# A two-layer hybrid decoder trunk on one core: the SBUF pools laid out anew, so that weights, work slots and x tiles begin at multiples of 512 bytes

## Chip, cores and metric

One NeuronCore of a Trainium2 chip. The metric is the device time of one execution in microseconds (us), lower is better. The input is one sequence of 512 tokens with 1024 channels in float32, through two layers.

## What is computed

```python
c_act = jax.nn.silu(c)
for layer in range(DEPTH):                                   # 2
    mod = jnp.einsum('bd,de->be', c_act, w_mod[layer]) + b_mod[layer]
    shift1, scale1, gate1, shift2, scale2, gate2 = split(mod, 6)
    h = rms_norm(x, mix_norm_w[layer]) * (1.0 + scale1) + shift1
    proj = jnp.einsum('btd,de->bte', h, w_in[layer])
    y_a = deltanet_mixer(...); y_b = spatial_gating_mixer(...); y_c = dilated_attention_mixer(...)
    x = x + gate1 * jnp.einsum('bte,ed->btd', concat(y_a, y_b, y_c), w_out[layer])
    h = rms_norm(x, ffn_norm_w[layer]) * (1.0 + scale2) + shift2
    gate, up = split(jnp.einsum('btd,df->btf', h, w_ffn_in[layer]), 2)
    x = x + gate2 * jnp.einsum('btf,fd->btd', jax.nn.silu(gate) * up, w_ffn_out[layer])
```

## The kernel before

x lies transposed in SBUF: eight tiles `xs` of [128 channels, 512 tokens]. Every operand of a large matmul is kept as two float32r parts, high (rounded) and low (the rest), and one product takes three matmuls: high by high, high weights by low x, low weights by high x. `mm3` (lines 548 to 552) issues these three, always in this order, on one bank of PSUM. A weight block is 128x128 and is the stationary operand; it is loaded anew before each of the three matmuls. The moving operand is a [128, 512] part of x.

Weights come from HBM in pieces, nearly all of [128, 1024], that is eight blocks of 128 columns (512 bytes per partition each). `loader` (line 429) issues their DMAs on SyncE into a ring of four `raw` tiles. `splitter` (line 473) makes the parts: ScalarE copies a piece to a `hi` tile, VectorE writes the difference to a `lo` tile. `hi` and `lo` are rings of three buffers each, so piece after piece goes round the three. `wcols` (line 513) picks a block of a piece. A few pieces, those for which `piece` has a `loose` number, are split into work slots instead of the ring.

Work slots are 58 equal tiles of [128, 512] float32 (`Arena`, line 240). They hold the parts of x, the results on their way, and everything else of that size. In a projection (`group`, `channels`) the moving operand is a slot and the stationary one a block of a ring buffer. In `proj_n` (line 1401) it is the other way round: a token block of a slot is stationary and 512, 256 or 264 columns of a ring buffer are moving. In `last_tiles` (line 652) both are slots, and the moving operand is half a slot, 256 columns.

The order of the instructions is made by a planner: tasks run against a rough model of the engines' time, and each engine's instructions are noted in that order. All have the source line 233. Names of tiles: `w` is a slot, `hi`, `lo`, `raw` the rings, `cst` the constants, `b` a PSUM bank, `s` a small tile. The profile writes a matmul as `b<-moving,stationary`.

Where the tiles lie follows from the order of the pools and the sizes of their tiles. In the program before, the pool `keep` (x, constants) comes first, then `par` (small tiles), then the slots and the rings. The slots begin at byte 62,112 of a partition and are 2,048 bytes apart, so every slot begins 160 bytes beyond a multiple of 512. A buffer of a ring is as large as its largest piece (1,056 columns, 4,224 bytes, that is 128 bytes more than a multiple of 512), so the three buffers differ:

| buffer of the ring | `hi` begins at, mod 512 | `lo` begins at, mod 512 | a slot begins at, mod 512 |
|---|---|---|---|
| first | 160 | 32 | 160 |
| second | 288 | 160 | 160 |
| third | 416 | 288 | 160 |

Blocks inside a piece are 512 bytes apart, so all blocks of a buffer have its offset. The constants begin at 128 mod 512.

Of the kernel before, what the change touches and what calls it, by code (L numbers as in the profile page):

```python
# [9 lines left out]
F32 = mybir.dt.float32  # L10
# [7 lines left out]
P = 128  # L18
T = 512
D = 1024  # L20
# [8 lines left out]
# columns of the constants array  # L29
C_ID, C_ONES, C_TRIU, C_TRIL, C_SLOW, C_BD, C_M64, C_M128, C_MG0, C_MPI, C_COS, C_SIN, C_RM = (  # L30
    0, 128, 256, 384, 512, 640, 768, 896, 1024, 1280, 1536, 1600, 1664)
C_N = 1665

# columns of the per-layer parameters array
L_BMOD, L_NW, L_CONV, L_ALOG, L_DTB, L_ONW, L_WC, L_RW, L_RWS = 0, 48, 64, 112, 116, 120, 121, 123, 155
L_N = 187

N_SLOTS = 58
N_RAW, N_RING = 4, 3
# [6 lines left out]
# the ranks of the tasks in layer 0 and after (the lowest goes first), the slack of an engine's queue, the free slots that  # L46
# weights kept apart from the ring ask for, and the banks that a projection leaves free
# [16 lines left out]
# the projections in the order of the mixers' use (in layer 0, k and q come first), and their pieces of w_in  # L64
# [9 lines left out]
# The kernel is written as tasks (generators), which run against a rough model of the engines' time, so that each  # L74
# engine's instructions come in an order in which few have to wait. A task yields what its next step needs: an AP
# (its data written), a Flag or Task (done), a function (time, or None while unknown), a tuple of these, or None.
# [10 lines left out]
class Plan:  # L87
# [21 lines left out]
    @staticmethod  # L109
    def span(ap):  # L110
        """the name of an AP's tensor, and its first and last column"""
        (step, _), free = ap.ap[0], ap.ap[1:]
        lo = ap.offset % step if ap.space != bass.MemoryType.DRAM and step else 0
        return ap.tensor.name, lo, lo + sum((n - 1) * s for s, n in free)
# [108 lines left out]
class Engine:  # L223
    """an engine whose instructions are noted in the plan"""
# [15 lines left out]
class Arena:  # L240
    """Equal tiles, the one that has been free longest first."""
# [22 lines left out]
    def need(self, n):  # L264
        """what a task yields that needs n of them"""
        return lambda: self.free[n - 1][0] if len(self.free) >= n else None


class Pair:
    """the float32 parts (high, low) of a [128, 512] operand; ok: written, by halves of the tokens"""  # L270
# [11 lines left out]
def _trunk(ctx, tc, xT, cb, consts, prm, gmp, wmod, wt, wn, wab, wo, wo2, wf1, wf2, out):  # L282
# [5 lines left out]

    keep = ctx.enter_context(tc.tile_pool(name="keep", bufs=1))
    par = ctx.enter_context(tc.tile_pool(name="par", bufs=1))  # L290
    wk = ctx.enter_context(tc.tile_pool(name="wk", bufs=1))
    wp = ctx.enter_context(tc.tile_pool(name="wp", bufs=4))
# [11 lines left out]
    def slots(n, spare=0):  # L304
        """n slots, as soon as they and some more are free"""
        yield arena.need(n + spare)
        return [slot() for _ in range(n)]

    def bank(n=1, spare=0):
        """n banks of psum, as soon as they and some more are free"""  # L310
        yield banks.need(n + spare)
        got = [banks.get() for _ in range(n)]
        return got[0] if n == 1 else got
# [14 lines left out]
    def heads(ap, n, w):  # L328
        """[128, n] as [128, n, w], each value w times"""
        return ap.rearrange("p (h o) -> p h o", o=1).to_broadcast([P, n, w])  # L330

    def every(ap, n, w):
        """[128, w] as [128, n, w], n times"""
# [45 lines left out]
    # pieces in the order of their use: columns of w_mod, and weights, which are split into float32 parts  # L379
# [5 lines left out]
    for l in range(depth):  # L385
# [9 lines left out]
        for k, (w, i) in enumerate(p for name in ORDER[min(l, 1)] for p in PIECES[name]):  # L395
            piece(w, l, i, 4 * 264 if w == "ab" else 1024, LOOSE["t"] if w == "t" and i < 3 else 0)
# [24 lines left out]
    def ring(tag, n, dt, bufs):  # L421
        t = wp.tile([P, n], dt, tag=tag, name=nm(tag), bufs=bufs)
# [4 lines left out]
        return t  # L427
# [25 lines left out]
    def modulation():  # L453
        """the entries of the modulation, in the order of their weights"""
# [44 lines left out]
    def take(*key):  # L499
        """the parts of the next weights"""  # L500
# [12 lines left out]
    def wcols(w, j, n=128):  # L513
        if isinstance(w[0], list):
            return wcols((w[0][j * n // T], w[1][j * n // T]), j % (T // n), n)
        return w[0][:, j * n:(j + 1) * n], w[1][:, j * n:(j + 1) * n]
# [5 lines left out]
    def rsqrt(v, n):  # L522
        """v ** -0.5 on [128, n] (v > 0): an integer start, then a step of third and one of second order"""
# [12 lines left out]
    def split(src, pair):  # L536
        """the float32 parts of a slot, which is freed"""
# [10 lines left out]
    def mm3(ps, w, x, first, last):  # L548
        """ps += w.T @ x by the float32 parts; w, x: (high, low)"""
# [4 lines left out]
    def operand(x, cols):  # L554
        """waits for an operand's columns"""
# [5 lines left out]
    def group(ws, rhs, cols, pss, order=range(KC)):  # L561
        """pss[j] = j-th weights.T @ rhs, chunk by chunk"""
# [6 lines left out]
    def tile_t(key, rhs):  # L569
        """psum of one column tile"""  # L570
# [6 lines left out]
    def tiles_t(keys, rhs):  # L577
        """psums of some column tiles together, by halves of the tokens"""
# [10 lines left out]
    def inv_rms(a, b0, n, warm=None):  # L589
        """psum with the inverse rms of x in every row, for n blocks of tokens from b0"""  # L590
# [17 lines left out]
    def norm_half(a, h, gg, l, which, half):  # L608
        """h = (high, low) of rms_norm(x) * w * (1 + scale) + shift, for half of the tokens"""
# [25 lines left out]
    def residual(c, ps, gate, cols, a):  # L635
        """x += gate * ps, and its squares"""
# [12 lines left out]
    def last_tiles(cs, w, where, rhs, gates, before, a, l, which):  # L649
        """the last chunks of a projection to x, by halves of the tokens, each with the norm that follows;  # L650
        returns its parts. where(c, k): which of the weights w, and which of its columns"""
# [34 lines left out]
    def conv(ps, ti, cw, func):  # L686
        """silu of the causal convolution of a projection, from psum; func: Silu, or Tanh and halved taps in cw
        (which needs no other table than Exp)"""
# [17 lines left out]
    def sumsq_heads(tiles):  # L706
        """[128 tok, (blk, h)] of the sums of squares over the 128 channels of each head, plus EPS"""
# [23 lines left out]
    def gates(ab, pr):  # L731
        """ab: [128, blk, 8] with a (4), b (4); returns g and beta, [128, (blk h)]"""
# [15 lines left out]
    def decay(c, g):  # L748
        """exp of the sums of g between the tokens of chunk c, lower triangles, (h, 128)"""
# [13 lines left out]
    def triangle(c, kT, s1, E, bc4):  # L763
        """B, the strictly lower part of the chunk's system (its upper part isn't zero)"""
# [17 lines left out]
    def blocks(l, bc, Bs):  # L782
        """inverses of the 32 x 32 diagonal blocks of I + B, compact: [128, (chunk h), 32]"""
        yield tuple(Bs)
        yield bc
        # one diagonal block per partition, forward substitution on the identity
        Q.dma_start(out=bscr[l].rearrange("n b i j -> (b i) n j"), in_=bc.rearrange("p (n j) -> p n j", j=32))
        free(bc)
        # and one half of the columns of its inverse: the even ones, the odd ones
# [28 lines left out]
    def dn_attn(c, qT, kT, E, B):  # L818
        """transposes of the decayed products of queries and keys of chunk c"""
# [21 lines left out]
    def dn_values(vT, h, bv):  # L841
        """beta * |k|^-1 * v of one head, [128 tok, (chunk, 128)]"""
# [15 lines left out]
    def dn_inverse(c, B, xc):  # L858
        """transposes of (I + B)^-1 of chunk c"""
# [39 lines left out]
    def k_decayed(c, kT, eg):  # L899
        """keys of chunk c, [128 tok, (h, 128)], decayed to its end"""  # L900
# [9 lines left out]
    def dn_chunk_out(c, qT, vt, AT, St, eg, oss):  # L910
        """o of chunk c, [128 tok, (h, 128)], and the sums of its squares"""
# [28 lines left out]
    def dn_scan(qT, kT, vv, Rs, ATs, scales, oss):  # L940
        """returns the tasks of o per chunk"""
# [64 lines left out]
    def dn_norm(scan, oss, qss):  # L1006
        """o is q.(rest) without the query's norm: its scale, rsqrt(|q|^2 + EPS) / sqrt(128), goes into the EPS"""
# [33 lines left out]
    def gmlp(l, vg):  # L1041
        """vg: two slots of gelu(v), [128 tok, (2 blk, 256)]; returns what gelu(u) is multiplied by, transposed"""
# [44 lines left out]
    def gated(l, ub, ts, pair, h_done):  # L1087
        """pair = gelu(u) * what the other half gives for it"""
# [12 lines left out]
    def rope_tables(pr):  # L1101
        """cos * w and sin * w (halves exchanged, first negative) for q and k; columns for the other channels"""
# [12 lines left out]
    def sw_in(b, ps, ss):  # L1115
        """a block of q and k from psum, and the sums of squares of its heads"""
# [11 lines left out]
    def sw_qk(xin, ss, gi, tables):  # L1128
        """four blocks [128 tok, q 256 | k 256]; returns -q.T / 8 per head pair and k.T per head, zero padded;
        patterns 1, 2: tokens in the order of t % 4"""  # L1130
# [93 lines left out]
    def attention(part, qk, vals, ml):  # L1224
        """part 0: blocks of tokens in order, keys of the block before and its own, pattern 0;
        part 1: blocks of one residue of t % 4, keys of the block for pattern 1 and for pattern 2.
        Scores are negated. ml: (minimum, sum) [128, (b h 2)]; returns the unnormalised outputs, transposed,
        per head pair"""
# [26 lines left out]
    def merge(l, mls, atts, pairs, last):  # L1255
        """one softmax over the keys of all patterns. (minimum, sum) go to the other part's order of tokens:
        token = 128 b + p in part 0, 4 p + r in part 1"""
# [57 lines left out]
    def first():  # L1315
        """layer 0: h chunk by chunk as the modulation comes, and with it the projections of k and q"""
# [4 lines left out]
        def warm(t, n=1):  # L1321
            """the tensor engine's clock rises with its load"""
# [62 lines left out]
    def layer(l, h, kq):  # L1385
        """the mixers; returns what goes into the channel mixer"""
# [14 lines left out]
        def proj_n(keys, width, tok):  # L1401
            """psum per block of tokens, [128 tok, width]; keys: (key, chunks of d in it)"""
            pss = None
            k = 0
            for key, n in keys:
# [3 lines left out]
                for j in range(n):  # L1409
                    wj = wcols(w, j, width)  # L1410
# [70 lines left out]
        def scales_of(gt, kss):  # L1481
            """decays to and from each token and over each chunk; beta / |k|, beta / |k|^2, and its product"""
# [106 lines left out]
        # output projection  # L1589
# [142 lines left out]
def _pack(inp):  # L1732
# [18 lines left out]
        rep(qw[:, :16]), rep(kw[:, :16]), rep(qw[:, swap]), rep(kw[:, swap]),  # L1751
    ], axis=2)
# [13 lines left out]
    # in layer 0, k and q run together: a piece per chunk of d  # L1766
# [32 lines left out]
```

## Time and profile before

| | |
|---|---|
| time, median of 3 runs | 1504.33 us (1503.94 to 1507.3) |
| span of the profiled execution | 1501.6 us |
| TensorE (PE) busy | 1478.1 us, 98% of the span, 7810 matmul records |
| weight loads (PEld) busy | 1235.6 us, 82% |
| VectorE (DVE) busy | 886.5 us, 59% |
| ScalarE (ACT) busy | 593.2 us, 40% |
| mean granted TensorE clock | 0.998 |
| DMA | 178.96 MB, queue busy 36.6% of 16 engines |

The profiled execution is known by its span alone, from its first to its last instruction; it lies 2.7 us below the median of the times. A matmul's duration in the profile is from its start to its modelled end, and one begins before the other has ended, so the pace of TensorE is read from starts, not from durations. An fp32 matmul has two records, an fp32r one has one; a row that says "f32" gives the type as the record has it, for both.

### The profile page before, as it was taken

The numbers are of one execution on the slowest core, as the hardware profiler recorded it, in microseconds if no ns is written. First come the engines' busy times: TensorE is split into PE (matmuls) and PEld (weight loads), VectorE is DVE, ScalarE is ACT, GpSimd is POOL, SyncE is SP. The second block draws the span as 40 slices with busy tenths as digits, with TensorE's granted clock in tenths as the row PEclk, the third lists the DMA queues.
The fourth block names the chain that finished last, engine by engine and source line by source line (L and its number), as shares of the span: only waits on it lengthen the run. The fifth ranks groups of instructions, "written<-read, shape, count | busy, mean of one in ns | idle before, by whom it ended". The sixth has DMA issues, their size and how long they took to land.

```text
span 1501.6 us, 19988 instructions
## 1 busy us (share of the span) xinstructions
PE 1478.1 (98%) x7810; PEld 1235.6 (82%) x7810; DVE 886.5 (59%) x1836; ACT 593.2 (40%) x1047; POOL 41.6 (3%) x60
## 2 busy tenths in 40 slices
PE   7999999999999999999999999999999999999998
PEld 5777998888988888888897889978788888888887
DVE  7787887946855555555476787656476333333332
ACT  4484326574432212222345623546544222122221
POOL 0001000000000000000000300100000000000000
PEclk9999999999999999999999999999999999999999
DMA  8723443404166555555322232121141223222231
GB/s 292 258 78 112 128 152 120 142 19 150 61 216 186 186 189 195 185 187 175 110 92 75 67 108 55 43 85 36 52 141 57 92 90 98 98 89 94 98 106 49
DMA packets 70638, 178.96 MB, mean 119 GB/s; under 512 B 25104, under 2 KB 25744, under 8 KB 70544
## 3 DMA queue, kind: packets, MB, share of 16 engines
q1 hardware_dynamic: 70544, 177.69, 36.6%
q8 instruction: 61, 1.00, 0.3%
q14 instruction: 33, 0.27, 0.1%
HBM read 174.45 MB, written 3.21 MB: 118 GB/s over the span
## 4 chain that ended last, share of the span: by engine, by line
PE 97%; DVE 1%; DMA 1%; ACT 1%; issue 0%; SPq 0%; ACTq 0%; DVEq 0%
PE b L233 97%; DMA raw<-in_wt_dram 0%; ACT w L233 0%; DVE w L233 0%; DMA xs<-in_xT_dram 0%; DVE raw L233 0%; SPq L233 0%; DVE s L233 0%; DVE xs L233 0%; ACT hi L233 0%; DVE lo L233 0%; DVE mod L233 0%; ACTq L233 0%; DVEq L233 0%
## 5 line engine op out<-in xcount | busy, mean ns | idle before, releaser
L233 PE MATMUL b<-w,hi 128*128 128x512 f32 (+1 forms) x2748 | 854.1, 392 | 2.5 <-ACT w L233 1.6
L233 PEld LDWEIGHTS b<-w,hi 128*128 128x128 f32 x2748 | 512.0, 189 | 123.8 <-issue 6.7
L233 PE MATMUL b<-w,lo 128*128 128x512 f32 (+1 forms) x1374 | 540.4, 393 | 0.0
L233 ACT ACTIVATE hi<-raw 128x1024 fp32r<-128x1024 f32 (+2 forms) x215 | 222.3, 1036 | 617.8 <-PE b L233 420.5
L233 DVE TENSOR_TENSOR lo<-raw,hi 128x1024 fp32r<-128x1024 f32 (+2 forms) x215 | 257.7, 1200 | 268.0 <-ACT hi L233 264.9
L233 PEld LDWEIGHTS b<-w,lo 128*128 128x128 f32 x1374 | 258.0, 188 | 54.7
L233 PE MATMUL b<-w,w 128*128 128x128 f32 (+2 forms) x1808 | 214.8, 284 | 4.0 <-ACT w L233 2.6
L233 PE MATMUL b<-hi,w 128*128 128x512 f32 (+2 forms) x768 | 215.0, 367 | 3.3 <-ACT w L233 3.3
L233 PEld LDWEIGHTS b<-w,w 128*128 128x128 f32 (+1 forms) x1808 | 199.2, 182 | 20.7 <-ACT w L233 10.6
L233 ACT ACTIVATE w<-b 128x512 f32<-128x512 f32 (+1 forms) x221 | 117.9, 559 | 137.0 <-PE b L233 126.0
L233 PEld LDWEIGHTS b<-hi,w 128*128 128x128 f32 x768 | 145.8, 211 | 26.0 <-issue 6.0
L233 PE MATMUL b<-lo,w 128*128 128x512 f32 (+2 forms) x384 | 137.7, 359 | 0.0
L233 DVE TENSOR_TENSOR w<-w,b 128x512 f32<-128x512 f32 x68 | 46.7, 687 | 131.8 <-PE b L233 131.0
L233 DVE CUSTOM_DVE_ANT_0 raw<-raw,cact,pr 128x1024 f32<-128x1024 f32 x96 | 122.3, 1279 | 0.5 <-DMA raw<-in_wmod_dram 0.5
L233 ACT ACTIVATE w<-w 128x512 f32<-128x512 f32 (+3 forms) x188 | 94.1, 520 | 23.0 <-DVE w L233 22.5
L233 PEld LDWEIGHTS b<-lo,w 128*128 128x128 f32 x384 | 80.7, 210 | 8.2
L233 DVE TENSOR_TENSOR w<-w,w 128x512 fp32r<-128x512 f32 (+2 forms) x104 | 68.1, 661 | 27.1 <-ACT w L233 18.1
L233 DVE SCALAR_TENSOR_TENSOR xs<-b,mod,xs 128x512 f32<-128x512 f32 (+1 forms) x56 | 37.1, 672 | 58.4 <-PE b L233 58.2
L233 PE MATMUL b<-cst,w 128*128 128x128 f32 (+1 forms) x416 | 57.6, 271 | 0.6 <-DVE w L233 0.6
L233 PEld LDWEIGHTS b<-cst,w 128*128 128x128 f32 x416 | 49.3, 145 | 8.4 <-issue 1.0
L233 DVE SCALAR_TENSOR_TENSOR w<-w,cw,w 128x509 f32<-128x509 f32 (+2 forms) x72 | 52.7, 766 | 0.9 <-ACT w L233 0.2
L233 ACT ACTIVATE w<-w,mod 128x256 fp32r<-128x256 f32 (+1 forms) x56 | 29.8, 539 | 48.6 <-DVE w L233 48.6
(85 smaller groups left out, 651.7 us busy)
## 6 DMA issues: line engine op xcount, KB each, us to landing
raw<-in_wf_dram SPq DMA_DIRECT2D x132, 512.0 KB, 3.8
raw<-in_wmod_dram SPq DMA_DIRECT2D x96, 512.0 KB, 3.4
raw<-in_wt_dram SPq DMA_DIRECT2D x36, 512.0 KB, 3.4
raw<-in_wn_dram SPq DMA_DIRECT2D x36, 512.0 KB, 3.3
raw<-in_wo_dram SPq DMA_DIRECT2D x16, 320.0 KB, 2.9
raw<-in_wo_dram SPq DMA_DIRECT2D x6, 512.0 KB, 3.3
raw<-in_wab_dram SPq DMA_DIRECT2D x4, 528.0 KB, 5.7
xs<-in_xT_dram SPq DMA_DIRECT2D x8, 256.0 KB, 5.9
```

Of the source, the lines that this page charges most:

```text
L233: r = f(*args, **kw)
```

## The change

Three things. (1) The pools are opened in another order: a gap of 384 bytes, then the slots, then the rings, then x and the constants, then the small tiles. (2) All ring tiles become 1,152 columns wide (4,608 bytes, nine times 512), of which a piece uses its first 1,024, 640 or 1,088. (3) Widths are padded: the two `ab` pieces from 264 to 272 columns per chunk (the matmuls still read 264), the constants from 1,665 to 1,680 and the layer parameters from 187 to 192 columns. In the built program every slot, every buffer of the three rings, every 128-column block and every `xs` tile then begins at 0 mod 512, as do the constants. The instructions of each engine, their order, their waits and their sizes are the same in both programs, but for the widths named under (3). Comments are gone, which moves line numbers.

```diff
-C_N = 1665
+C_N = 1680
-L_N = 187
+L_N = 192
+N_PIECE, N_AB, GAP = 1152, 272, 96
...
+    gap = ctx.enter_context(tc.tile_pool(name="gap", bufs=1))
+    gap.tile([P, GAP], F32, name="gap")
+    wk = ctx.enter_context(tc.tile_pool(name="wk", bufs=1))
+    wp = ctx.enter_context(tc.tile_pool(name="wp", bufs=4))
     keep = ctx.enter_context(tc.tile_pool(name="keep", bufs=1))
     par = ctx.enter_context(tc.tile_pool(name="par", bufs=1))
-    wk = ctx.enter_context(tc.tile_pool(name="wk", bufs=1))
-    wp = ctx.enter_context(tc.tile_pool(name="wp", bufs=4))
...
-            piece(w, l, i, 4 * 264 if w == "ab" else 1024, LOOSE["t"] if w == "t" and i < 3 else 0)
+            piece(w, l, i, 4 * N_AB if w == "ab" else 1024, LOOSE["t"] if w == "t" and i < 3 else 0)
...
     def ring(tag, n, dt, bufs):
-        t = wp.tile([P, n], dt, tag=tag, name=nm(tag), bufs=bufs)
+        t = wp.tile([P, N_PIECE], dt, tag=tag, name=nm(tag), bufs=bufs)
...
-        return t
+        return t[:, 0:n]
...
-    def wcols(w, j, n=128):
+    def wcols(w, j, n=128, pitch=None):
         if isinstance(w[0], list):
             return wcols((w[0][j * n // T], w[1][j * n // T]), j % (T // n), n)
-        return w[0][:, j * n:(j + 1) * n], w[1][:, j * n:(j + 1) * n]
+        a = j * (pitch or n)
+        return w[0][:, a:a + n], w[1][:, a:a + n]
...
-                    wj = wcols(w, j, width)
+                    wj = wcols(w, j, width, N_AB if key[0] == "ab" else None)
...
+        np.zeros((L, P, L_N - L_RWS - 32), np.float32),
...
-    a["wab"] = wide(np.concatenate([w_in[:, :, 2312:2568], w_in[:, :, 2048:2056]], axis=2), 4)
+    a["wab"] = wide(np.concatenate([w_in[:, :, 2312:2568], w_in[:, :, 2048:2056],
+                                    np.zeros((L, D, N_AB - 264), np.float32)], axis=2), 4)
```

## Rows read from the trace of the kernel before

**Rows 1.** The page, share of the chain that ended last, and its clock in 40 slices

```profile
PEclk9999999999999999999999999999999999999999
...
PE 97%; DVE 1%; DMA 1%; ACT 1%; issue 0%; SPq 0%; ACTq 0%; DVEq 0%
```

**Rows 2.** Waits of PE: who waited for whom, us in total, times, longest

```profile
PE b L233 <- ACT w L233: 15.2, 11, 7.0
PE b L233 <- DVE w L233: 2.8, 6, 0.6
PE b L233 <- DVE s L233: 1.6, 2, 0.9
```

**Rows 3.** Groups by form, PE: shapes xcount | busy us, mean ns | idle before

```profile
L233 PE MATMUL b<-w,hi 128*128 128x512 f32 x2660 | 838.1, 396 | 2.5 <-ACT w L233 1.6 <-DVE w L233 0.9
L233 PE MATMUL b<-w,lo 128*128 128x512 f32 x1330 | 528.0, 397 | 0.0
L233 PE MATMUL b<-hi,w 128*128 128x512 f32 x512 | 165.5, 404 | 0.0
L233 PE MATMUL b<-w,w 128*128 128x256 f32 x768 | 102.5, 291 | 3.2 <-ACT w L233 1.9 <-DVE w L233 1.1
L233 PE MATMUL b<-lo,w 128*128 128x512 f32 x256 | 100.8, 394 | 0.0
...
L233 PE MATMUL b<-w,cst 128*128 128x512 f32 x16 | 7.4, 598 | 0.0
```

**Rows 4.** Windows, both FFNs: us, PE, PEld, DVE, ACT, POOL busy (x), PEclk, DMA, GB/s

```profile
416.00:738.00 322.00, 322.00 (x1389) 261.88 (x1388) 172.06 (x222) 84.42 (x103) 0.00 (x0) 1.00 0.56 182
1153.00:1490.00 337.00, 337.00 (x1454) 274.15 (x1453) 110.32 (x116) 84.32 (x101) 0.00 (x0) 1.00 0.28 92
```

**Rows 5.** Timeline, PE, starts of pieces (second, first, third, second buffer), both FFNs

```profile
582.29 0.63 PE L233 MATMUL b<-w,hi 128*128 128x512 f32 x2
582.75 0.40 PE L233 MATMUL b<-w,lo 128*128 128x512 f32 x1
...
587.89 0.62 PE L233 MATMUL b<-w,hi 128*128 128x512 f32 x2
588.35 0.40 PE L233 MATMUL b<-w,lo 128*128 128x512 f32 x1
...
593.44 0.62 PE L233 MATMUL b<-w,hi 128*128 128x512 f32 x2
...
598.99 0.63 PE L233 MATMUL b<-w,hi 128*128 128x512 f32 x2
...
1163.55 0.63 PE L233 MATMUL b<-w,hi 128*128 128x512 f32 x2
...
1169.16 0.62 PE L233 MATMUL b<-w,hi 128*128 128x512 f32 x2
...
1174.70 0.62 PE L233 MATMUL b<-w,hi 128*128 128x512 f32 x2
...
1180.26 0.63 PE L233 MATMUL b<-w,hi 128*128 128x512 f32 x2
```

**Rows 6.** Timeline, PE: a run in layer 1's mixers, and its last projection tiles by halves

```profile
848.41 2.74 PE L233 MATMUL b<-w,cst 128*128 128x512 f32 x6
...
1109.06 14.20 PE L233 MATMUL b<-w,w 128*128 128x256 f32 x117
```

**Rows 7.** Timeline, PE, a run of fp32 matmuls of 128 columns in the first mixers

```profile
223.48 5.52 PE L233 MATMUL b<-w,w 128*128 128x128 f32 x48
```

**Rows 8.** Groups by form, PE: the mean duration in that run

```profile
L233 PE MATMUL b<-w,w 128*128 128x128 f32 x736 | 89.9, 276 | 0.2 <-DVE w L233 0.2
```

**Rows 9.** The page, the split of a piece on ACT and DVE

```profile
L233 ACT ACTIVATE hi<-raw 128x1024 fp32r<-128x1024 f32 (+2 forms) x215 | 222.3, 1036 | 617.8 <-PE b L233 420.5
L233 DVE TENSOR_TENSOR lo<-raw,hi 128x1024 fp32r<-128x1024 f32 (+2 forms) x215 | 257.7, 1200 | 268.0 <-ACT hi L233 264.9
```

**Rows 10.** DMA issues on SyncE: count, KB each, median us to landing

```profile
raw<-in_wf_dram SPq DMA_DIRECT2D x132, 512.0 KB, 3.8
...
raw<-in_wab_dram SPq DMA_DIRECT2D x4, 528.0 KB, 5.7
```

## Prediction

> **What bounds the kernel now.** I read the chain of waits first: 97% of the span is PE, at the full granted clock in all 40 slices, which of its two levels is 2.4 GHz [rows 1]. Then the waits: PE waited 19.6 us in all for another engine [rows 2]. So the time is the number of matmuls times the pace at which PE starts them, and nothing else is worth much. The groups by form give the number: 2660 + 1330 + 512 + 256 = 4758 fp32r matmuls of 512 columns, and 768 of 256 columns with both operands in slots [rows 3]. The pace I take from starts. In two long windows of the channel mixers PE is busy without a hole; less the one instruction that runs in from before, 322.0 us / 1388 and 337.0 us / 1453 are both **232.0 ns a step** [rows 4]. 4758 such steps are 1104 us, 73% of the span. VectorE works 172 of 322 us there and ScalarE 84, so nothing but PE's own pace sets these stretches.
>
> The timeline then shows that this pace depends on where the weights lie. Four pieces in a row begin at 582.29, 587.89, 593.44 and 598.99 [rows 5]: 24 matmuls in 5.60 us, in 5.55 and in 5.55, that is 233.3, 231.3 and 231.3 ns a step. The three pieces have the same shapes, the same moving slots and no waits; what differs is the ring buffer. The slow one is the second, whose `hi` begins at 288 mod 512 and whose `lo` begins at 160; in layer 1 it is the second again, 5.61 us against 5.54 and 5.56 (1163.55 to 1180.26). So where the operands lie costs time here, and the change moves every one of them.
>
> **What the change does, part by part.** No instruction is added, removed or moved on any engine, and no wait changes. What is left is the pace of each instruction.
>
> *The 512-column steps.* After the change moving and stationary operand always begin at the same place mod 512, and so do one weight block and the next. No 512-column row of the trace has that in every step: in the first buffer two of three loads stand so to the moving slot, in the second one, in the third none. The nearest row that has it in all steps is the run of 117 matmuls with both operands in slots, the same three-matmul product on half slots: (14.20 us − 0.291) / 116 = 119.9 ns a step [rows 3, 6]. What the columns alone would take I get from fp32 matmuls of 512 columns, which step at (2.74 − 0.598) / 5 = 428 ns [rows 3, 6]; fp32r takes its columns at twice that rate, as the 232 ns show, so 512 columns are 214 ns and 256 are 107. With equal offsets 119.9 − 107 = 12.9 ns come on top of the columns, against 232.0 − 214 = 18 ns in the rings. I take the 12.9 for 512 columns too: 214 + 12.9 = 226.9, so a step falls by 5.1 ns.
>
> The bounds of this: above, the effect could be nothing or a loss (rivals); below, all 18 ns go and a step is 214. I stay at 226.9 because the slots' row is the one whose operands lie to each other as all will after. But its operands begin at 160, all of them, and what a start at 0 mod 512 is worth by itself no fp32r row shows, since in the rings and slots of before every operand begins 32 bytes beyond a multiple of 128. That can only be bounded, by the 214.
>
> By the Trainium skill ("TensorE: Matmul & The Clock Gate", section "Wait — 56ns, not 53.3ns?") a warm stream of 512-column matmuls steps at 215.7 ns, which the rows here do not reach; by that figure 16.3 ns would go per step, some 78 us in all (an estimate).
>
> *How much reaches the end.* In the two windows 1388 + 1453 = 2841 steps have no wait beside them [rows 4]: 2841 × 5.1 = 14.5 us, whole. The other 1917 steps lie in the mixers and projections, 9.8 us, among PE's waits for ACT and DVE [rows 2]. A faster PE there comes sooner to the same results, and the wait that grows is the one for ACT's `w` (15.2 us now). I take three quarters, 7.4 us; none and all would be 0 and 9.8. Sum: 21.9 us.
>
> *The 256-column steps between slots* keep their operands' places to each other. Nothing by the forecast. Their bound is the shortest step seen with a full weight load, (5.52 − 0.276) / 47 = 112 ns for 128 columns [rows 7, 8]: 768 × 8 = 6 us at most.
>
> *The splits.* One piece takes ScalarE 1.04 us and VectorE 1.20 us [rows 9], in 5.6 us of PE's time; their operands move as well. If both slowed by a tenth, 0.22 us more per piece would still fit three times over; cover gone would mean a piece over 5.5 us, and nothing is near that. The four `ab` pieces are 3% wider: 0.03 × (1.04 + 1.20) = 0.07 us each, and their transfer, now 5.7 us [rows 10], 0.2 us. The padded constants and parameters are one or two transfers each, issued a piece's time and more ahead. I cost all of it at nothing; uncovered it would be under 1.1 us. The other loads keep their size and their 3.8 us.
>
> So the span is 1501.6 − 21.9 = 1479.7 us, and with the 2.7 us by which this execution lies under the median, **1482 us**.
>
> **The rivals.**
>
> *Deeper.* The start at 0 mod 512 counts by itself, and steps go towards 214. All of it: 4758 × 18 = 86 us, with the 256-column steps 92, which gives 1412; half of it about 1458. For it: the fp32 matmul has its 512 columns in 428 ns, with a moving slot at 160 and its weights in the constants, which begin at 128 mod 512, and the excess in the rings is there at every offset tried. Against it: none of the offsets in the trace comes near, and fp32 takes its columns at half the pace, where a clash of two readers would hide.
>
> *Nothing.* Where the weights begin does not matter to a running matmul, and the 0.05 us of the second buffer has another cause, or only that goes: 0.05 us per 72 steps is 0.7 ns a step, 3.3 us in all. That is 1501 to 1504. Against it: the same buffer is slow in both layers, with VectorE at 172 of 322 us and at 110 of 337 [rows 4, 5]. A rule says the same as this rival: by the Trainium skill ("TensorE: Matmul & The Clock Gate", section "Step-by-step: what each phase is for") loading the next tile's weights takes no SBUF bandwidth from the running matmul, since each has a read port of its own. By that rule the time stays at 1504; the trace does not agree, by 5.60 against 5.55 us.
>
> *Slower.* Equal offsets are what is dear: the weight load then begins in step with the moving operand and both want the same place at once. For it: the slow second buffer is the only one whose `lo` begins where the moving slot does. Its extra 0.05 us, put on its 8 `lo` loads, is 6.3 ns each; after the change all 24 loads stand so, 231.3 + 6.3 = 237.6 ns, which is 5.6 × 4758 = 27 us more: 1531. It decides from the point where the mean step rises over 232. Against it: the first buffer's `hi`, 16 of 24 loads, stands so too and is not slow, and the slots' run has it in every step at 12.9 ns over its columns.
>
> **How the numbers follow.** A measurement of this kernel tells about 0.2%, 3 us, from no change. Forecast 0.45, its own range 1470 to 1496 (2 to 7 ns a step); deeper 0.24 (1412 to 1470); nothing 0.14; slower 0.17 (1508 to 1531). Faster is the first two, 0.69. The range reaches from 1416, which leaves out only the end of the deeper case, to 1510, which takes in "nothing" and the mildest end of "slower"; some 0.17 is outside.
>
> **What would show it.** In the profile after, the same two windows' kind of stretch (us over count less one): 227 ns is the forecast, 214 to 221 the deeper case, 231 or 232 nothing, over 233 slower. The starts of pieces must come evenly, with no third piece longer than the other two, since the three buffers are then alike. The run of 256-column steps should stay at 120; if it falls, the absolute start counts. PE's waits for ACT should grow by a few us at most; if they grow by as much as the steps gain, the mixers were bound by ACT after all. The forecast is wrong if the step is over 230 or under 223.

## The result, and the profile after

The changed kernel takes 1484.28 us (median of 4 runs, 1483.93 to 1484.94) against 1504.17 us for the kernel before in the same job (4 runs): ratio 0.9865, 95% interval 0.9851 to 0.9879. That is 2.3 us from the 1482 forecast. The profiled execution has a span of 1482.5 us, where before had 1501.6.

The page of the changed kernel, the busy times of its engines and the chain that ended last:

```profile
PE 1460.3 (99%) x7810; PEld 1235.4 (83%) x7810; DVE 886.4 (60%) x1836; ACT 593.5 (40%) x1047; POOL 40.7 (3%) x60
...
PE 97%; DVE 1%; ACT 1%; DMA 0%; issue 0%; SPq 0%; ACTq 0%; DVEq 0%
```

Nothing of the shape has changed: as many matmuls, and PE is still 97% of the chain, as in [rows 1]. What changed is PE's own busy time.

Where the 19.1 us of span went is read from starts. Both programs issue the same 7810 matmul records in the same order, so each interval from one start to the next has its partner in the other trace. The intervals that begin with a 512-column matmul lost **20.25 us**: 15.26 in the two channel mixers (2839 intervals) and 4.99 in the rest (1918). All others together gave back 2.07 us, and the first matmul starts 0.92 us earlier: 20.25 − 2.07 + 0.92 = 19.1. (The groups of [rows 3] do not give this: their busy times overlap, and the modelled durations change with the pace.)

Part of what was given back, and of what the rest lost too little, is the clock's. PE in two windows of the changed kernel (us; PE busy with its count; granted clock, DMA share, GB/s):

```profile
24.00:26.00 2.00, 2.00 (x6) 0.52 0.84 291
72.00:79.00 7.00, 6.60 (x29) 0.52 0.23 75
```

The same two windows of the kernel before:

```profile
24.00:26.00 2.00, 2.00 (x11) 1.00 0.89 334
72.00:79.00 7.00, 6.39 (x40) 0.76 0.03 11
```

In the first, eight 512-column steps of the changed kernel took 408 to 427 ns each, at the lower of the two levels (1.2 GHz), where the kernel before needed 227 to 234. Followed matmul by matmul, the changed kernel fell behind by 1.6 us there and by another 0.8 us in the second window, 2.4 us in all. Just ahead of the first, PE was busy 1.8 of 4 us in the changed kernel and 1.7 of 4 us in the kernel before, whose clock stayed up; no run shows that the change brings this about. The page's 40 slices are too wide to show it.

PE's waits (who waited for whom, us in total, times, longest):

```profile
PE b L235 <- ACT w L235: 14.5, 12, 6.1
PE b L235 <- DVE w L235: 2.2, 5, 0.6
PE b L235 <- DVE s L235: 1.6, 2, 0.9
```

They sum to 18.3 us against 19.6 in [rows 2]; 0.9 of these 1.3 us is the wait ahead of the first matmul, 6.1 instead of 7.0 us. PE's busy time as a whole fell by 1478.1 − 1460.3 = 17.8 us, and with the 1.3 us of waits that is the 19.1 us again.

The pace, in windows inside the two channel mixers of the changed kernel (us; PE, PEld, DVE, ACT, POOL busy with their counts; clock, DMA share, GB/s):

```profile
420.00:720.00 300.00, 300.00 (x1325) 248.48 (x1324) 163.71 (x210) 81.56 (x99) 0.00 (x0) 1.00 0.60 189
...
1170.00:1460.00 290.00, 290.00 (x1282) 240.19 (x1281) 98.33 (x103) 74.36 (x89) 0.00 (x0) 1.00 0.30 97
```

300 us / 1324 = 226.6 ns and 290 us / 1281 = 226.4 ns a step, where [rows 4] gave 232.0. The clock column is 1.00 in both kernels, so the 5.4 ns are not the clock's. And the pieces on the timeline of the changed kernel's PE (start, busy us of the merged row), each row the first of a piece:

```profile
1152.17 0.61 PE L235 MATMUL b<-w,hi 128*128 128x512 f32 x2
...
1157.62 0.61 PE L235 MATMUL b<-w,hi 128*128 128x512 f32 x2
...
1163.05 0.62 PE L235 MATMUL b<-w,hi 128*128 128x512 f32 x2
```

They come every 5.45 and 5.43 us, against 5.60 in the slow buffer and 5.55 in the two others of [rows 5]. Two operations that should not move did not. First the run of 256-column steps between slots, cut by its window; then, on the page, the split of a piece:

```profile
1098.04 8.20 PE L235 MATMUL b<-w,w 128*128 128x256 f32 x67
```

```profile
L235 ACT ACTIVATE hi<-raw 128x1024 fp32r<-128x1024 f32 (+2 forms) x215 | 222.6, 1037 | 600.2 <-PE b L235 414.8
L235 DVE TENSOR_TENSOR lo<-raw,hi 128x1024 fp32r<-128x1024 f32 (+2 forms) x215 | 258.9, 1206 | 258.9 <-ACT hi L235 258.1
```

With the mean duration of 291 ns, the same in both kernels, (8.20 − 0.291) / 66 = 119.8 ns, as before the 119.9 of [rows 6]; the splits take 1037 and 1206 ns against 1036 and 1200 in [rows 9].

### The profile page after: what moved, and what is told of

Same layout as the page of the kernel before. It is cut to its first block, busy times and chain, and to the rows that moved or that the text cites. A ratio compares the mean times of both kernels' runs of the same rounds, so it can differ in the third digit from the quotient of the medians.

```text
span 1482.5 us, 19988 instructions
## 1 busy us (share of the span) xinstructions
PE 1460.3 (99%) x7810; PEld 1235.4 (83%) x7810; DVE 886.4 (60%) x1836; ACT 593.5 (40%) x1047; POOL 40.7 (3%) x60
## 4 chain that ended last, share of the span: by engine, by line
PE 97%; DVE 1%; ACT 1%; DMA 0%; issue 0%; SPq 0%; ACTq 0%; DVEq 0%
PE b L235 97%; DVE w L235 1%; ACT w L235 1%; DMA xs<-in_xT_dram 0%; DVE s L235 0%; DVE raw L235 0%; DVE xs L235 0%; SPq L235 0%; DVE lo L235 0%; DVE mod L235 0%; ACT hi L235 0%; ACTq L235 0%; DVEq L235 0%
## 5 line engine op out<-in xcount | busy, mean ns | idle before, releaser
L235 PE MATMUL b<-w,hi 128*128 128x512 f32 (+1 forms) x2748 | 844.5, 389 | 2.5 <-ACT w L235 1.6
L235 PE MATMUL b<-w,lo 128*128 128x512 f32 (+1 forms) x1374 | 531.2, 387 | 0.0
L235 ACT ACTIVATE hi<-raw 128x1024 fp32r<-128x1024 f32 (+2 forms) x215 | 222.6, 1037 | 600.2 <-PE b L235 414.8
L235 DVE TENSOR_TENSOR lo<-raw,hi 128x1024 fp32r<-128x1024 f32 (+2 forms) x215 | 258.9, 1206 | 258.9 <-ACT hi L235 258.1
```

Source lines behind the costliest of these rows:

```text
L235: r = f(*args, **kw)
```

## The experiments

The time fell as forecast, but the change does two things at once. It makes all ring buffers 1152 columns wide, so that every piece stands to the moving operand at the same place; and it lays the pools out so that this place is a multiple of 512 bytes. My theory was that only the first counts: the distance between where the stationary block and the moving operand begin, taken modulo some power of two. The rival was that starting at a multiple of 512 counts by itself. Both parts were then run alone, and after that the distance was varied. Below, "distance" is the start of the stationary block less that of the moving operand, in bytes modulo 512 unless another modulus is named; a piece is 24 steps, so its length over 24 is the step. A step runs from the start of one matmul to the start of the next, and the weights of that next one are loaded beside it.

**The ring width alone**, on the kernel before, with its pools in their old order (everything then begins at 160 mod 512):

```diff
-        t = wp.tile([P, n], dt, tag=tag, name=nm(tag), bufs=bufs)
+        t = wp.tile([P, 1152], dt, tag=tag, name=nm(tag), bufs=bufs)
...
-        return t
+        return t[:, 0:n]
```

> The kernel before with one part of the change alone: ring tiles 1152 columns wide, pools in their old order. Slots, hi and lo then all begin at 160 mod 512, so every operand lies to every other as in the changed kernel, but 160 bytes off a multiple of 512. Theory A (only the offsets of the operands to each other mod 512 count): the clean 512-column step is 227 ns as in the changed kernel, pieces take 5.44 us in all three buffers, time 1482 to 1487. Theory B (the start at 0 mod 512, or mod 128, counts by itself): the step stays near 232 ns, time 1500 to 1506.

Measured: 1483.04 us (4 runs, 1482.74 to 1484.01), ratio to before 0.9857, interval 0.9842 to 0.9872. The starts of its pieces on PE:

```profile
1172.36 0.62 PE L233 MATMUL b<-w,hi 128*128 128x512 f32 x2
...
1177.80 0.62 PE L233 MATMUL b<-w,hi 128*128 128x512 f32 x2
...
1183.24 0.62 PE L233 MATMUL b<-w,hi 128*128 128x512 f32 x2
```

5.44 us each, 226.7 ns a step, with no operand at a multiple of 512. The ring width alone gives the whole gain.

**The pool order alone**: the changed kernel with its slots at 0 mod 512, but ring tiles as narrow as before, so that the three buffers of `hi` begin at 0, 256 and 128 and those of `lo` at 384, 128 and 0:

```diff
-N_PIECE, N_AB, GAP = 1152, 272, 96
+N_PIECE, N_AB, GAP = 1152, 264, 96
...
-        t = wp.tile([P, N_PIECE], dt, tag=tag, name=nm(tag), bufs=bufs)
+        t = wp.tile([P, n], dt, tag=tag, name=nm(tag), bufs=bufs)
...
-        return t[:, 0:n]
+        return t
```

> The other part alone: the changed kernel's order of pools and gap, with the ring tiles as wide as before (1056 columns). Slots begin at 0, hi at 0, 128 and 256, lo at 384, 0 and 128: the same places to each other as before, all moved down by 160 bytes, so that every operand begins at a multiple of 128. Theory A: steps as before, 231 ns in two buffers and 233.5 in the one whose hi is at 128, mean 232, time 1500 to 1506. Theory B (a start at a multiple of 128): 227 ns, time 1482 to 1490.

Measured: 1505.89 us (10 runs), ratio 1.0002, interval 0.9992 to 1.0012. Its pieces on PE:

```profile
1171.24 0.62 PE L235 MATMUL b<-w,hi 128*128 128x512 f32 x2
...
1176.79 0.62 PE L235 MATMUL b<-w,hi 128*128 128x512 f32 x2
...
1182.34 0.63 PE L235 MATMUL b<-w,hi 128*128 128x512 f32 x2
...
1187.95 0.62 PE L235 MATMUL b<-w,hi 128*128 128x512 f32 x2
```

5.55, 5.55 and 5.61 us: the three lengths of the kernel before [rows 5], although the slots and the first buffer of `hi` begin at 0 mod 512. The rival has fallen; the new pool order is worth nothing by itself.

**Which distances are quick.** Two kernels give `hi` and `lo` rings of their own whose buffers are 1168 columns wide, so that each begins 64 bytes on from the one before (distances 0, 64, 128; then 192, 256, 320, with another gap ahead):

```diff
-N_PIECE, N_AB, GAP = 1152, 272, 96
+N_PIECE, N_AB, GAP = dict(raw=1152, hi=1168, lo=1168), 272, 96
...
-    wp = ctx.enter_context(tc.tile_pool(name="wp", bufs=4))
+    wps, GAPS = {}, dict(hi=0, lo=80)
+    for tag in ("raw", "hi", "lo"):
...
+        wps[tag] = ctx.enter_context(tc.tile_pool(name="w" + tag, bufs=4))
```

> The changed kernel with hi and lo in rings of their own whose buffers begin at 0, 64 and 128 mod 512; hi and lo of one piece alike, so that inside a piece one weight load always begins where the last did. Slots at 0. Theory A1 (the weights' offset to the moving operand counts): 227 ns a step (pieces 5.44 us) in the buffer at 0, more in those at 64 and 128, some 232 to 234 at 128. Theory A2 (what counts is that one load begins where the last one did): 227 ns in all three buffers, time as the changed kernel, 1482 to 1487.

> The same with the buffers at 192, 256 and 320 mod 512. Theory A1: the step differs by buffer, 227 at 256 if 256 is as good as 0 (before, hi at 256 from the slot was among the two quick buffers), 230 to 238 at 192 and 320; a value under 227 would show that 0 is not the best place. Theory A2: 227 ns in all three.

Three more (32, 96, 160; 224, 16, 240; 176, 200, 208) keep the changed kernel's buffers and let a piece begin so many bytes into its own:

```diff
+SHIFT = dict(raw=(0, 0, 0), hi=(32, 96, 160), lo=(32, 96, 160))
...
-        return t[:, 0:n]
+        at = SHIFT[tag][uses[tag] % 3] // 4
+        uses[tag] += 1
+        return t[:, at:at + n]
```

> The changed kernel with pieces that begin 32, 96 and 160 bytes into their ring buffers, hi and lo of a piece alike, slots at 0. So far 0 and 256 gave 227 to 228 ns a step, 192 gave 229, and 64, 128 and 320 gave 233. Theory A1 with a period of 256 (a clash of two readers at one place): a smooth curve, 32 between 227 and 233, 96 and 160 at 233 or a little under. If the step at 32 is already 233, only places very near 0 are good; if it is under 226.7, 0 is not the best place.

> The same with 224, 16 and 240 bytes. Theory A1 with a period of 256: 224 (32 below 256) between the 229 of 192 and the 227 of 256, 16 and 240 within 1 to 3 ns of 227. If something finer than 64 bytes counts (a line of 32 or 64 bytes that is straddled), 16 and 240 are dearer than 32 and 224. Time of this kernel 1483 to 1495.

> The changed kernel with pieces 176, 200 and 208 bytes into their buffers, around 192, which gave 229 ns with single steps down to 226. If 192 lies on the edge of a place better than 0, one of these is under 226.7 ns, and a kernel that has it everywhere would beat both. If 0 and 256 are the only good places, all are 229 to 234 and the time is 1495 to 1512.

Measured, one run each: 1500.19, 1497.16, 1512.44, 1497.78 and 1503.45 us, with the kernel before at 1505.01 (first two), 1505.57 (next two) and 1505.36 in the same jobs. Starts of pieces on PE's timeline, in the order of use; first the kernel with 0, 64 and 128 (here 128, 64, 0):

```profile
1172.64 0.64 PE L235 MATMUL b<-w,hi 128*128 128x512 f32 x2
...
1178.23 0.63 PE L235 MATMUL b<-w,hi 128*128 128x512 f32 x2
...
1183.83 0.62 PE L235 MATMUL b<-w,hi 128*128 128x512 f32 x2
...
1189.29 0.64 PE L235 MATMUL b<-w,hi 128*128 128x512 f32 x2
```

The kernel with 192, 256 and 320 (320, 256, 192):

```profile
1171.25 0.63 PE L235 MATMUL b<-w,hi 128*128 128x512 f32 x2
...
1176.85 0.62 PE L235 MATMUL b<-w,hi 128*128 128x512 f32 x2
...
1182.32 0.62 PE L235 MATMUL b<-w,hi 128*128 128x512 f32 x2
...
1187.81 0.63 PE L235 MATMUL b<-w,hi 128*128 128x512 f32 x2
```

The kernel with 32, 96 and 160 (160, 32, 96):

```profile
1170.36 0.63 PE L236 MATMUL b<-w,hi 128*128 128x512 f32 x2
...
1175.96 0.63 PE L236 MATMUL b<-w,hi 128*128 128x512 f32 x2
...
1181.57 0.63 PE L236 MATMUL b<-w,hi 128*128 128x512 f32 x2
...
1187.18 0.63 PE L236 MATMUL b<-w,hi 128*128 128x512 f32 x2
```

The kernel with 224, 16 and 240 (16, 240, 224):

```profile
1173.51 0.61 PE L236 MATMUL b<-w,hi 128*128 128x512 f32 x2
...
1178.95 0.61 PE L236 MATMUL b<-w,hi 128*128 128x512 f32 x2
...
1184.40 0.63 PE L236 MATMUL b<-w,hi 128*128 128x512 f32 x2
...
1189.99 0.61 PE L236 MATMUL b<-w,hi 128*128 128x512 f32 x2
```

The kernel with 176, 200 and 208 (in this order):

```profile
1170.93 0.62 PE L236 MATMUL b<-w,hi 128*128 128x512 f32 x2
...
1176.44 0.63 PE L236 MATMUL b<-w,hi 128*128 128x512 f32 x2
...
1181.98 0.63 PE L236 MATMUL b<-w,hi 128*128 128x512 f32 x2
...
1187.55 0.62 PE L236 MATMUL b<-w,hi 128*128 128x512 f32 x2
```

Each difference of two starts is a piece:

| distance, bytes | piece, us | step, ns |
|---|---|---|
| 0, in the changed kernel | 5.44 | 227 |
| 16 / 240 | 5.44 / 5.45 | 227 / 227 |
| 256 | 5.47 | 228 |
| 192 / 176 | 5.49 / 5.51 | 229 / 230 |
| 200 / 208 | 5.54 / 5.57 | 231 / 232 |
| 224 / 128 | 5.59 / 5.59 | 233 / 233 |
| 64, 320 / 160 | 5.60 / 5.60 | 233 / 233 |
| 32 / 96 | 5.61 / 5.61 | 234 / 234 |

Three things follow. The pattern repeats after 256 bytes, not 512, in the pairs that were run: 256 is quick like 0, 320 is as dear as 64, and 384 as dear as 128 (`lo` in two buffers of the kernel with the pool order alone, both 5.55 us). Within 16 bytes of a multiple of 256 a step costs 227 to 228 ns, at most other places about 233; between 176 and 208 it lies between the two, rising again to 233 at 224. And no place beats 0. Theory A2 has fallen too: in the buffers at 64 and 128 every load begins where the last one did, and the step is 233 ns. Not all of this was expected: a smooth curve did not come, for 32 is as dear as 96 and 224 is not between 192 and 256, and so the kernel with 224, 16 and 240 took 1497.78 us and not 1483 to 1495.

In the kernel with 0, 64 and 128 the piece at 0 takes 5.46 us, not 5.44. The starts of single matmuls in the trace, which the timeline's rows merge, show where the difference lies (means over 44 pieces): the first three steps, behind a dear piece, take 228.7, 232.1 and 230.8 ns, the last, beside which the first block of the next dear piece is loaded, 232.5, and those between 226.7. In the piece at 256 the first six steps take 228 to 235 ns and the others 226 to 227, like those at 0. So some steps behind a dear piece are dear although their own weights are well placed; why they are three in the one and six in the other is open.

**One operand of two.** `hi` at 0, and `lo` alone at 256, 128 and 64:

```diff
+SHIFT = dict(raw=(0, 0, 0), hi=(0, 0, 0), lo=(256, 128, 64))
```

> The changed kernel with hi always at 0 and lo 256, 128 or 64 bytes into its buffer. Theory A1 alone (each load costs by its own offset to the moving slot): the two loads of hi cost 227 ns whatever lo does, so a piece steps at 227 (lo at 256), 229 (128) and 229 (64). Theory A1 with A2 (it costs as well that a load begins elsewhere than the one before): loads of hi after lo, and of lo after hi, cost 232 to 234 although hi is at 0, as in the first buffer of the kernel before, and pieces step at 230 to 232 even with lo at 256.

Measured: 1496.21 us. Its pieces on PE (`lo` at 128, 64, 256):

```profile
1170.71 0.62 PE L236 MATMUL b<-w,hi 128*128 128x512 f32 x2
...
1176.26 0.61 PE L236 MATMUL b<-w,hi 128*128 128x512 f32 x2
...
1181.80 0.62 PE L236 MATMUL b<-w,hi 128*128 128x512 f32 x2
...
1187.26 0.62 PE L236 MATMUL b<-w,hi 128*128 128x512 f32 x2
```

5.55, 5.54 and 5.46 us. If only the eight steps of `lo` were dear, a piece would be 16 × 226.7 + 8 × 233.3 ns = 5.49 us. With two dear steps for each load of `lo` it is 8 × 226.7 + 16 × 233.3 ns = 5.55 us, and that was measured. Single starts show which two (`lo` at 128, means over 46 pieces): the step between the two matmuls with `hi` takes 226.8 ns, the next, beside which `lo` is loaded, 232.4, and the one of the matmul that uses `lo` 234.2. So a load at distance 128 makes dear both the step beside it and the step that uses it. (This is not so at each distance: the last step of the pieces at 224, with a block at 16 loaded beside it, takes 226.6 ns.) That two loads in a row begin at different places costs nothing by itself in the two cases that the traces hold: with `lo` at 256 and `hi` at 0 the steps settle at 226.4 to 226.8 ns, and the step from the piece at 16 to that at 240 takes 227.0. This is also why the buffers of the kernel before are all slow. The first and the third have `lo` off by 128 modulo 256, as here: 5.55 us, the same. The second has `hi` off by 128 and `lo` in place: two loads of three dear, and with their neighbours all three, 5.60 us.

**Is it the amount that is loaded?** If a misplaced load delays the running matmul by taking something from it, and the 13 ns that stay over the columns are such a delay too, then a load of 64 or 32 columns should cost less than one of 128. In the first half of the second channel-mixer product, chunks 1 to 9 of 11 use only the first 64 weight columns in layer 0, and 32 in layer 1; the second of the two kernels also moves every piece to distance 128:

```diff
-                    mm3(ps, wcols(w[p], n), x, k == 0, k == KH - 1)
+                    m = (64, 32)[l] if 0 < k < KH - 1 and not half else P
+                    mm3(ps[0:m], tuple(a[:, 0:m] for a in wcols(w[p], n)), x, k == 0, k == KH - 1)
```

> The changed kernel, but in the first half of the FFN's second matrix the matmuls of chunks 1 to 12 of 14 load only 64 of a block's 128 weight columns in layer 0 and 32 in layer 1, so half or three quarters of those outputs' sums are left out. The moving operand keeps its 512 columns. If the 13 ns over the columns belong to the weight load that runs beside the matmul, the step falls with the load's width: 220 ns with 64 columns, 217 with 32. If they belong to the matmul itself (its 512 columns, its bank of PSUM), it stays at 227 in both.

> The same narrow loads with all pieces 128 bytes into their buffers, where full loads stepped at 232.7 ns. If the dear offset costs by what the load reads, its extra 6 ns fall as well: 223 ns with 64 columns, 218 with 32. If an offset costs once per matmul, the steps are 226 and 223. The rest of the kernel shows 233 ns, time 1500 to 1512.

(The 12 of 14 chunks there is a miscount: it is 9 of 11, runs of 27 matmuls.) Measured: 1486.24 us, and 1506.16 with all pieces at 128. In the first kernel the loads did become shorter; its groups by form, PE's weight loads:

```profile
L235 PEld LDWEIGHTS b<-w,hi 128*128 128x128 f32 x2460 | 454.7, 188 | 100.3 <-issue 6.7 <-DVE w L235 2.4 <-ACT w L235 2.0
...
L235 PEld LDWEIGHTS b<-w,hi 128*64 128x64 f32 x144 | 19.4, 135 | 13.2
...
L235 PEld LDWEIGHTS b<-w,hi 128*32 128x32 f32 x144 | 15.7, 109 | 17.1
```

The step did not. On PE's timeline of the same kernel, the first row of a narrow run and the first one behind it, for 64 columns and for 32:

```profile
510.46 0.63 PE L235 MATMUL b<-w,hi 128*64 128x512 f32 x2
...
516.67 0.63 PE L235 MATMUL b<-w,hi 128*128 128x512 f32 x2
...
1240.44 0.63 PE L235 MATMUL b<-w,hi 128*32 128x512 f32 x2
...
1246.70 0.63 PE L235 MATMUL b<-w,hi 128*128 128x512 f32 x2
```

6.21 and 6.26 us for 27 steps are 230 and 232 ns, three and five more than with the full load. At distance 128, the same two rows for 32 columns on that kernel's PE:

```profile
1256.08 0.61 PE L236 MATMUL b<-w,hi 128*32 128x512 f32 x2
...
1262.31 0.62 PE L236 MATMUL b<-w,hi 128*128 128x512 f32 x2
```

That is 6.23 us, 231 ns (the run with 64 columns: 6.20 us, 230 ns). Both alternatives that I had put up missed: the step does not fall with the load, neither from 227 nor from 233, and a load whose weight block is narrow costs about the same at 0 and at 128. The 13 ns over the columns do not shrink with the amount loaded; what they are, and why a full load at 0 is the cheapest of all that were tried, these runs do not say. The narrow matmuls also write fewer rows of their bank, which was not tried apart.

**Steps of 256 columns.** The kept traces also hold fp32r matmuls of 256 columns whose moving operand is a ring piece. The same stretch of layer 0 in three kernels, 10 us each: the kernel before (distances 0 and 128 modulo 256 mixed), the second kernel with narrow loads (all at 128; none of its loads is narrow here), and the changed kernel (all at 0), in this order:

```profile
269.00:279.00 10.00, 10.00 (x87) 1.00 0.59 201
...
271.00:281.00 10.00, 10.00 (x87) 1.00 0.58 200
...
269.00:279.00 10.00, 10.00 (x86) 1.00 0.66 211
```

From starts, 95 steps in a row take 118.8, 118.5 and 119.9 ns each. At 256 columns a distance of 128 is not dear, and 0 is not cheaper. The fp32 matmuls of 512 columns with weights in the constants do not show the pattern either: 429 ns at 224 in the kernel before and 429 ns at 0 after.

## Why the prediction was right, step by step

- *The 512-column step* was put at 226.9 ns from the 256-column run's 12.9 ns over its columns. The windows show 226.6 and 226.4 (before they were 232.0 and 231.9). The mechanism was right: how the operands stand to each other decides, and not the absolute start, as the ring width by itself shows (1483.04 us, 226.7 ns at 160 mod 512). The split into columns and a rest also holds: 226.6 − 119.8 = 106.8 ns for 256 columns leaves 13 ns over 512 of them. But that the size came out so near was luck in part. The slots' row was chosen because its operands stand at equal offsets, and steps of 256 columns take 118.5 to 119.9 ns whether they stand so or not; the row could not tell what equal offsets are worth.
- *How much reaches the end.* For the two channel mixers, 2841 steps × 5.1 ns = 14.5 us; starts give 15.3. For the other 1917 steps I took three quarters of 9.8 us, 7.4. This term was too large: 19.1 − 15.3 = 3.8 us came from outside the channel mixers: these steps lost 5.0, and the others gave some of it back. I had expected PE's waits to swallow the missing quarter, and that reason was wrong, since the waits fell from 19.6 to 18.3 us. The traces show two others. The steps there that nothing interrupts fell by 3.7 ns and not 5.1 (6.5 us in 1770 steps; 3.1 ns in the 724 of them whose moving operand is the ring piece), and why is open. And 2.4 us went to the lower clock at 24 and at 72 us. At equal clocks the span would have fallen by some 21.5 us (an estimate, 19.1 + 2.4), close to the 21.9 of the sum; there the first term was too small and the second too large, which is luck again.
- *The 256-column steps* stayed at 119.8 ns, and the splits at 1037 and 1206 ns. Both terms were zero, and right. (Of the 768 records counted as steps between slots, 720 are fp32r; the others belong to fp32 matmuls. With a term of zero this changes nothing.)
- *Deeper* had 0.24. It rested on the start at 0 mod 512 counting by itself. The pool order alone (ratio 1.0002) and the ring width alone (0.9857, against 0.9865 with both) refute it.
- *Nothing* had 0.14: the place of the weights would not matter to a running matmul. Refuted most plainly by two kernels that do the same arithmetic, with the same rings, waits and loads: 1512.44 us with the pieces at 32, 96 and 160, 1484.28 with them at 0, each in a job with before at 1504 to 1506. The Trainium skill ("TensorE: Matmul & The Clock Gate", section "Step-by-step: what each phase is for") has this rival's rule, that loading the next weights takes no SBUF bandwidth from the running matmul; the measured steps of 227 and 233 ns at one clock do not agree with a load that costs the matmul nothing, but whether bandwidth is what it loses no run shows.
- *Slower* had 0.17: equal starts would be the dear ones. It read the slow second buffer the wrong way round. There `lo` was in place and `hi`, two loads of three, was not. A misplaced load makes two steps dear, which is why the first buffer, with only `lo` misplaced, looked nearly as slow, and why the before kernel's rows could not settle which operand was to blame.

The 215.7 ns a step that the Trainium skill gives for a warm stream ("TensorE: Matmul & The Clock Gate", section "Wait — 56ns, not 53.3ns?") was reached by no 512-column step of any run here: the shortest single one took 223 ns, and the quickest of the long windows is 226.4 ns a step.

## What to carry to other kernels

Where PE is the bound by fp32r matmuls of 512 columns and its pieces differ in length by ring buffer with shape, clock and waits the same, look at the widths of the ring's buffers: make each a multiple of 256 bytes, and let moving and stationary operands begin at the same place modulo 256. That was a change of two lines here, and a new pool order on top of it brought nothing that can be measured (1483.04 against 1484.28 us). For steps of 256 columns nothing was gained. Check it on starts of pieces, since busy times of overlapping matmuls hide five ns in four hundred.

## What the runs showed of the hardware

- An fp32r matmul of 512 columns steps at 227 to 228 ns, as a mean over a piece, when its stationary block begins 0, 16, 240 or 256 bytes from the moving operand (modulo 512), and at 233 to 234 ns at 32, 64, 96, 128, 160, 224 and 320, at the same granted clock. At 176, 192, 200 and 208 it takes 230, 229, 231 and 232.
- A load at distance 128 slows both the step beside it and the step that uses it: 232.4 and 234.2 ns against 226.8, and `lo` alone misplaced costs 5.55 us a piece and not 5.49.
- Fp32r steps of 256 columns do not show the pattern: 118.5 ns with all distances at 128, 119.9 at 0. Nor do fp32 records of 512 columns: 429 ns at 224 and at 0.
- A load of half or a quarter of the columns makes the step no shorter, but 230 and 232 ns.
- Left open: by what mechanism the distance acts, what the fixed 13 ns a step are, why 256 columns escape, and how operands of other types behave, which no run here tried.
